# Hybrid encoder trunk on one core: first norm of the mixer row by row, and four other moves in the mixer's order of work

## The chip, the cores and the metric

One core of one Trainium2 chip runs the whole program once. The metric is device time in microseconds (us), the median of three runs. TensorE (PE in the rows) does matmuls, PEld its weight loads, VectorE is DVE, ScalarE is ACT, GpSimd is POOL, and SyncE (SP) issues the DMAs.

## The reference, cut to what matters

Two sequences (512 and 1024 rows of 1024 features) go through one layer: feed-forward, mixer, feed-forward, each followed by a residual and a layer norm. The mixer has three groups side by side: a gated recurrence (256 features), differential attention (4 heads), and a Fourier mixing (256 features).

```python
def encoder_trunk(x, ...):
    x = layer_norm(ALPHA * x + 0.5 * swiglu(x, ffn1_wg[l], ffn1_wu[l], ffn1_wd[l]), ln_g[l, 0], ln_b[l, 0])
    x = layer_norm(ALPHA * x + hybrid_mixer(x, w_in[l], ...), ln_g[l, 1], ln_b[l, 1])
    x = layer_norm(ALPHA * x + 0.5 * swiglu(x, ffn2_wg[l], ffn2_wu[l], ffn2_wd[l]), ln_g[l, 2], ln_b[l, 2])
def diff_attention(q, k, v, lam, subln_g, lam_init):
        s = jnp.einsum('bqhcd,bkhcd->bhcqk', qi, k) * scale + bias[None, :, None]
        p = jax.nn.softmax(s, axis=-1)
        w = p[:, :, 0] - lam * p[:, :, 1]
        return jnp.einsum('bhqk,bkhe->bqhe', w, v)
    o = o * lax.rsqrt(jnp.mean(o * o, -1, keepdims=True) + NORM_EPS) * subln_g * (1.0 - lam_init)
def fourier_mix(f):
    out = jnp.fft.fft2(fg, axes=(1, 3), norm='ortho').real
```

## The kernel before, in words

The rows are split into three chunks of 512: chunk 0 is the short sequence (q=0), chunks 1 and 2 are the long one (q=1). `ffn` runs before and after the mixer; the change touches only the mixer, which takes the span from about 1050 to 1745 us. Nearly all products are made in three passes of split operands: `mm3` (L139) issues three matmuls, and `split` makes a rounded part on ACT (L133) and the rest on DVE (L134).

**Two interleaved streams.** `attention` is a generator with one step per block of 128 queries: 16 blocks for q=0 (4 heads of 4), then 32 for q=1 (4 heads of 8). `others` is the second stream, a chain of generators: 18 steps left of the input projection `project` (each 24 matmuls of 128x512), mixed with the two Fourier generators `fnet` (7 and 12 steps), then `out_proj` of chunk 0, `first_norm`, and `out_proj` of chunk 1. `along` (L96) advances `others` after attention step n until its count of steps is at least `int(PACE(n))`. Before, PACE is 2 + 2.4 n up to n = 14 and grows by 0.8 a step from there. Step 0 comes before the first block, so n is also the block's number.

**One attention block** n: fill `ahead` with scores up to two blocks further (three in q=1; LOOK); one `next` on each tail of earlier `values`; `weigh` (L1061 to L1069) mixes both softmax maps and transposes the weights; then RATE[q] steps of the next head's `load` (8 in q=0, 1 in q=1); every second block starts a `values` tail. A load has seven DMAs of q, k and v. Scores are 8 matmuls (L1040, q=1), a bias and minimum on DVE (L1043) and an exp on ACT (L1045). A `values` tail has three steps, one a block: the product with v (L1077) and copies (L1080, L1081); column sums of squares (L1087), L1088 and a power on POOL (L1089); transposes of the result (L1093), the scaling (L1094), a split and the write to `y` in DRAM.

**The rest of the order.** `fnet` makes products with a channel table `ct`, then one group of 12 matmuls for each table tile; `table()` loads one tile ahead into one of two `r` slots. `out_proj(c)` loads eight tiles of `y` as soon as they are marked in `mixed` (else it yields a step that does nothing), then takes 16 steps of 24 matmuls. For chunk 0 it goes beside attention and writes its rows to `x1p` in DRAM. `first_norm` (one step) loads the four rows of `x1p` into `x` slots and calls `layer_norm` (L204): all four rows together on ACT, DVE and POOL, among them two `tensor_add` on POOL (L230). `layer_norm_row` (L236) is the row-wise form that the other norms use.

A planner places the instructions: on each engine it may put an instruction that it takes to be ready ahead of an earlier one. Tiles come from tagged slots (`xt` 6, `w` 5, `x` 6, `a` 5, `p`, `b`, `d`, `r` 2, `m` 4); a new tile waits until a slot of its tag is free, its DMA on SP's queue among others. "any" walks through a, x and p (13 slots), "any_b" alternates b and d. PSUM has three `big` and two `mm` slots in the mixer. The two score maps of a block and a projection step both take `big`.

Of the kernel before, what the change touches and what calls it, by code (L numbers as in the profile page):

```python
# [20 lines left out]
P = 128  # L21
# [18 lines left out]
FIRST = 30  # L40
PACE = lambda n: 2 + 2.4 * n + max(0, n - 14) * (0.8 - 2.4)
AHEAD = {(q, h): 2 + ((q, h) == (9, 2)) for q in range(2) for h in range(HEADS)}
RATE = (8, 1)
STORE = lambda nc, t: nc.sync
FN = 256
BATCH = 4
POOLED = lambda t: t % 2 == 0
MIXER = lambda nc, q, qb: nc.vector
# [26 lines left out]
def f32(ap):  # L75
    return ap.bitcast(F32)
# [27 lines left out]
class Kernel:  # L104
# [93 lines left out]
    def ln_params(self, i, tag):  # L198
# [3 lines left out]
        return ps  # L202

    def layer_norm(self, rows, sums, params, dst=None, part=range(TPC)):  # L204

        nc = self.nc
        for t0 in part[::BATCH]:
            ts = range(t0, min(t0 + BATCH, part.stop))
            n = len(ts)
            st = self.tiny("st", [3, TPC])[:, :, :n]  # L210
            mean, var, rs = (st[:, i] for i in range(3))
            if sums.shape[2] > 1:
                nc.vector.tensor_reduce(mean, sums[:, t0:t0 + n], axis=mybir.AxisListType.X, op=ALU.add)
                nc.vector.tensor_scalar(mean, mean, -1.0 / D, None, op0=ALU.mult)
            else:
                nc.vector.tensor_scalar(mean, sums[:, t0:t0 + n, 0], -1.0 / D, None, op0=ALU.mult)
            for t in ts:
                k = t - t0
                nc.scalar.activation(self.slot("a", [D], BF16), rows[t], AF.Square, bias=mean[:, k:k + 1],
                                     accum_out=var[:, k:k + 1])  # L220
            nc.vector.tensor_scalar(var, var, 1.0 / D, EPS / ALPHA ** 2, op0=ALU.mult, op1=ALU.add)
            nc.gpsimd.tensor_tensor(rs, var, self.mhalf[:, :n], op=ALU.pow)
            for t in ts:
                a, k = rows[t], t - t0
                nc.vector.scalar_tensor_tensor(a, a, mean[:, k:k + 1], params[0], op0=ALU.add, op1=ALU.mult)  # L225
            for t in ts:
                a, k = rows[t], t - t0
                if POOLED(t):
                    nc.scalar.activation(a, a, AF.Identity, scale=rs[:, k:k + 1])
                    nc.gpsimd.tensor_add(a, a, params[1])  # L230
                else:
                    nc.vector.scalar_tensor_tensor(a, a, rs[:, k:k + 1], params[1], op0=ALU.mult, op1=ALU.add)  # L232
                if dst is not None:
                    STORE(nc, t).dma_start(dst[t], a)

# [749 lines left out]
    def attention(self, blocks, dist, others):  # L985
# [85 lines left out]
        def values(q, h, qc):  # L1071
            NB = SEQS[q] // P
            zz, wt = chunks.pop((q, h, qc))
            vv = packs[q, h][2]
            po = self.psum("mm", [QC])
            for kb in range(NB):
                nc.tensor.matmul(po, vv[:, kb, :], wt[:, kb, :], start=kb == 0, stop=kb == NB - 1)  # L1077
            o = self.slot("any_b", [2, QC])
            o, sq = o[:, 0], o[:, 1]
            nc.scalar.copy(o, po)  # L1080
            nc.scalar.square(sq, po)  # L1081
            ms = self.tiny("ms", [2, JQ])
            nc.vector.scalar_tensor_tensor(ms[:, 0], zz[:, :, 0], EPS, zz[:, :, 0], op0=ALU.mult, op1=ALU.mult)
            yield
            pb = self.psum("mm", [QC])
            for j in range(JQ):
                nc.tensor.matmul(pb[:, j:j + 1], sq[:, j * P:(j + 1) * P], self.ones, start=True, stop=True)  # L1087
            nc.vector.scalar_tensor_tensor(ms[:, 0], pb[:, 0:JQ], 1.0 / P, ms[:, 0], op0=ALU.mult, op1=ALU.add)  # L1088
            nc.gpsimd.tensor_tensor(ms[:, 1], ms[:, 0], self.mhalf[:, 0:JQ], op=ALU.pow)  # L1089
            yield  # L1090
            pb = self.psum("mm", [QC])
            for j in range(JQ):
                nc.tensor.transpose(pb[:, j * P:(j + 1) * P], ms[:, 1, j:j + 1].to_broadcast([P, P]), self.ident)  # L1093
            nc.vector.scalar_tensor_tensor(o, o, self.subg, pb, op0=ALU.mult, op1=ALU.mult)  # L1094
            y = self.slot("any_b", [2, QC], F32R)
            self.split(y[:, 0], y[:, 1], o)
            nc.sync.dma_start(f32(self.scr["y", q, 2 + h])[:, :, qc * QC:(qc + 1) * QC].rearrange("a p s -> p a s"), f32(y))
            self.mixed[q, 2 + h, qc * QC] = 1
# [6 lines left out]
        for n, block in enumerate(blocks):  # L1105
            q, h, qb = block
            i = heads.index((q, h))
            while len(ahead) <= LOOK[q] and n + len(ahead) < len(blocks):
                block = blocks[n + len(ahead)]
                run(loads[heads.index(block[:2])])  # L1110
                ahead.append(scores(*block))
            for tail in tails:
                next(tail, None)
# [11 lines left out]
    def fnet(self, q, S):  # L1125
# [3 lines left out]
        H, N = S // 2, FN  # L1129
        ct = self.slot("any", [2, 2 * P], F32R)  # L1130
        nc.sync.dma_start(f32(ct), f32(self.scr["chan", q]).rearrange("a p n -> p a n"))
# [21 lines left out]
        else:  # L1153
            abs_ = self.slot("xt", [2, 2, S // P, 2 * P], F32R)
            abs_ = [abs_[:, cb] for cb in range(2)]
        abs_ = [[ab[:, l] for l in range(2)] for ab in abs_]
        for cb in range(2):
            fs, ab = ahead, abs_[cb]
# [8 lines left out]
        ys = [[self.slot("any", [S], F32R) for _ in range(2)] for _ in range(2)]  # L1167
        parts = fourier_parts(S)
        order = [t for tiles, _, _ in parts for t in tiles]
        tabs = []  # L1170

        def table():
            if order:
                tabs.append(self.slot("r", [2, 2, N], F32R))
                nc.sync.dma_start(f32(tabs[-1]), f32(self.scr["dft", q])[order.pop(0)])

        table()
        for tiles, sl, mirror in parts:
            if mirror:
                pss = [self.psum("mm", [2, N]) for _ in range(2)]  # L1180
            else:
                both = self.psum("mm", [2, N])
                pss = [both[:, cb:cb + 1] for cb in range(2)]
            for t in tiles:
                table()
                tab = tabs.pop(0)
                for cs in range(2):
# [22 lines left out]
    def out_proj(self, c, src, accs, beside=None):  # L1210
# [4 lines left out]
        if beside:  # L1215
            pairs = [self.slot("w", [2, 2, CH], F32R) for _ in range(2)]
            four = self.slot("xt", [KD // 2, 2, CH], F32R)
            yt = [p[:, i] for p in pairs for i in range(2)] + [four[:, i] for i in range(4)]
        else:
# [102 lines left out]
    def mixer(self, project, x1, x2, x1p, chunk):  # L1322
# [16 lines left out]
        def first_norm():  # L1339
            self.layer_norm(self.load_rows(x1p, "x"), self.sums[:, 0], self.ln_params(1, "x"), chunk(x2, 0))  # L1340
            yield

        def begun(steps):
# [4 lines left out]
        others = Steps(islice(project, 15), begun(fnets[0]), project, islice(fnets[0], 3), begun(fnets[1]), *fnets,  # L1348
                       self.out_proj(0, chunk(x1, 0), None, beside=x1p), first_norm(),
                       self.out_proj(1, chunk(x1, 1), accs[1]))  # L1350
        along(self.attention(blocks[0] + blocks[1], dist, others), others, PACE)
# [68 lines left out]
```

## Time and profile before

| | us |
|---|---|
| median of 3 runs (2820.43 to 2826.11) | 2821.38 |
| the profiled execution's own time | 2823.13 |
| its span, first to last instruction | 2821.3 |
| PE busy (97%) | 2739.7 |
| DVE busy (68%) | 1920.5 |
| ACT busy (41%) | 1153.8 |
| POOL busy | 104.6 |

Busy time is a share of the whole span; a stage's limit is read from the windows. "<-" in a wait names what ended it. PEclk is TensorE's granted clock as a share of full speed; in single stretches it is 1.00 (2.4 GHz) or 0.5 (1.2 GHz), and a window shows the mean.

### The profile page before, as it was taken

The numbers are of one execution on the slowest core, as the hardware profiler recorded it, in microseconds if no ns is written. First come the engines' busy times: TensorE is split into PE (matmuls) and PEld (weight loads), VectorE is DVE, ScalarE is ACT, GpSimd is POOL, SyncE is SP. The second block draws the span as 40 slices with busy tenths as digits, with TensorE's granted clock in tenths as the row PEclk, the third lists the DMA queues.
The fourth block names the chain that finished last, engine by engine and source line by source line (L and its number), as shares of the span: only waits on it lengthen the run. The fifth ranks groups of instructions, "written<-read, shape, count | busy, mean of one in ns | idle before, by whom it ended". The sixth has DMA issues, their size and how long they took to land. (4 is left out here: it accounts for less than half of the span.)

```text
span 2821.3 us, 39205 instructions
## 1 busy us (share of the span) xinstructions
PE 2739.7 (97%) x14940; PEld 2505.0 (89%) x14940; DVE 1920.5 (68%) x3218; ACT 1153.8 (41%) x2155; POOL 104.6 (4%) x104
## 2 busy tenths in 40 slices
PE   7999999999999999999988989999999999999998
PEld 7998999899999987987867979999999999999997
DVE  7677767686767773453477774877776668676677
ACT  5344434333323243663356562544433334232323
POOL 2000000010000010000000010000000001000001
PEclk9999999999999999999999999999999999999999
DMA  7799866888655573225577566488876577555553
GB/s 248 262 303 313 296 244 248 308 297 270 239 194 194 180 234 106 96 103 168 168 229 194 154 215 235 162 293 272 303 276 239 216 291 283 194 187 189 199 181 111
DMA packets 302284, 627.40 MB, mean 222 GB/s; under 512 B 22544, under 2 KB 178832, under 8 KB 283152
## 3 DMA queue, kind: packets, MB, share of 16 engines
q1 hardware_dynamic: 298096, 618.09, 63.7%
q0 software_dynamic: 4000, 6.82, 0.9%
q8 instruction: 117, 1.92, 0.3%
q14 instruction: 71, 0.58, 0.1%
HBM read 388.90 MB, written 235.93 MB: 221 GB/s over the span
## 5 line engine op out<-in xcount | busy, mean ns | idle before, releaser
L139 PE MATMUL up<-xt,a 128*128 128x384 f32 x4032 | 734.0, 337 | 2.9 <-DVE xt L134 2.1
L139 PEld LDWEIGHTS up<-xt,a 128*128 128x128 f32 x4032 | 701.8, 188 | 13.5 <-DVE xt L134 2.8
L139 PE MATMUL up<-xt,w 128*128 128x384 f32 x3360 | 617.5, 337 | 0.0
L139 PEld LDWEIGHTS up<-xt,w 128*128 128x128 f32 x3360 | 588.8, 188 | 21.4 <-ACT t L462 8.9
L139 PE MATMUL big<-w,h 128*128 128x512 f32 x1584 | 387.3, 393 | 1.9 <-ACT h L133 1.6
L586 DVE SCALAR_TENSOR_TENSOR x<-big,x 128x512 f32<-128x512 f32 x420 | 278.9, 685 | 107.1 <-PE big L139 104.3
L139 PEld LDWEIGHTS big<-w,h 128*128 128x128 f32 x1584 | 295.0, 188 | 60.7 <-ACT h L133 3.4
L139 PE MATMUL big<-a,h 128*128 128x512 f32 x1260 | 319.9, 395 | 2.4 <-ACT h L133 2.4
L139 PEld LDWEIGHTS big<-a,h 128*128 128x128 f32 x1260 | 234.9, 189 | 44.1 <-ACT h L133 2.8
L139 PE MATMUL big<-xt,w 128*128 128x512 f32 x1008 | 235.0, 392 | 5.8 <-issue 2.7
L533 DVE SCALAR_TENSOR_TENSOR x<-big,x 128x1024 f32<-128x1024 f32 (+1 forms) x156 | 177.2, 1139 | 87.0 <-PE big L139 86.9
L139 PEld LDWEIGHTS big<-xt,w 128*128 128x128 f32 x1008 | 189.2, 189 | 47.3 <-issue 3.1
L134 DVE TENSOR_TENSOR a<-w,a 128x512 fp32r<-128x512 f32 x244 | 164.4, 688 | 70.4 <-ACT a L133 65.7
L133 ACT CAST a<-w 128x512 fp32r<-128x512 f32 x244 | 148.0, 621 | 25.7 <-DMA w<-in_ffn_wg 11.9
L134 DVE TENSOR_TENSOR a<-b,a 128x512 fp32r<-128x512 f32 x176 | 121.5, 694 | 42.4 <-ACT a L133 39.8
L133 ACT CAST a<-b 128x512 fp32r<-128x512 f32 x176 | 108.6, 620 | 97.0 <-PE up L139 38.9
L133 ACT CAST h<-t 128x384 fp32r<-128x384 f32 x168 | 86.1, 513 | 125.8 <-DVE t L516 79.7
L139 PE MATMUL mm<-w,xt 128*128 128x256 f32 x960 | 122.2, 286 | 0.1
L139 PEld LDWEIGHTS mm<-w,xt 128*128 128x128 f32 x960 | 118.4, 193 | 0.6 <-DVE x L1244 0.5
L512 ACT ACTIVATE t<-t 128x384 f32<-128x384 f32 x132 | 69.3, 525 | 81.4 <-DVE t L457 42.1
L462 ACT COPY t<-up 128x384 f32<-128x384 f32 x84 | 40.3, 479 | 152.0 <-PE up L139 151.9
L443 DVE TENSOR_TENSOR t<-t,up 128x384 f32<-128x384 f32 x84 | 46.3, 552 | 82.2 <-ACT t L442 82.1
(329 smaller groups left out, 3046.6 us busy)
## 6 DMA issues: line engine op xcount, KB each, us to landing
left<-a SPq DMA_DIRECT2D x280, 512.0 KB, 4.2
w<-left SPq DMA_DIRECT2D x136, 1024.0 KB, 4.7
w<-in_ffn_wg SPq DMA_DIRECT2D x23, 1024.0 KB, 5.6
w<-in_ffn_wu SPq DMA_DIRECT2D x23, 1024.0 KB, 7.6
d<-in_ffn_wd SPq DMA_DIRECT2D x88, 256.0 KB, 4.3
x<-x SPq DMA_DIRECT2D x44, 512.0 KB, 4.1
ops<-a SPq DMA_DIRECT2D x42, 512.0 KB, 3.6
w<-in_ffn_wd SPq DMA_DIRECT2D x20, 1024.0 KB, 5.0
```

The source lines that it names most:

```text
L133: self.nc.scalar.copy(hi, src)
L134: self.nc.vector.tensor_sub(lo, src, f32(hi))
L139: self.nc.tensor.matmul(out, lhs(l), rhs(r), start=first and n == 0, stop=last and n == 2, skip_group_check=onto)
L443: nc.vector.tensor_add(s, s, b)
L462: nc.scalar.copy(s2 := quarter(), a)
L512: nc.scalar.activation(g, x, AF.Silu)
L533: nc.vector.scalar_tensor_tensor(accs[t][:, at], pd, scale, accs[t][:, at], op0=ALU.mult, op1=ALU.add, **acc)
L586: nc.vector.scalar_tensor_tensor(x, ps, scale, x, op0=ALU.mult, op1=ALU.add)
```

## The change

1. `first_norm` uses the row-wise norm, one row loaded ahead into `m` slots, and advances one step for every step of `out_proj` of chunk 1 (`together`). 2. RATE of q=1 becomes 2. 3. Two Fourier tables are loaded ahead, in slots r, r, m, the first two before the channel products; `ct` moves from "any" to `m`. 4. The last step of a `values` tail comes one block later, and its two working tiles and its result share one "any_b" tile. 5. The three scores of the first block are separated by yields, and PACE starts with three slower steps. Besides, `out_proj` of chunk 0 takes four single slots (m, m, m, any) in place of one `xt` slot.

```diff
-PACE = lambda n: 2 + 2.4 * n + max(0, n - 14) * (0.8 - 2.4)
+RAMP = 3
+PACE = lambda n: 2 + min(n, RAMP) + 2.4 * max(0, n - RAMP) + max(0, n - RAMP - 14) * (0.8 - 2.4)
-RATE = (8, 1)
+RATE = (8, 2)
+TABLES = "rrm"
...
-    def layer_norm(self, rows, sums, params, dst=None, part=range(TPC)):
...
 def values(q, h, qc):
-            o = self.slot("any_b", [2, QC])
-            o, sq = o[:, 0], o[:, 1]
+            y = self.slot("any_b", [2, QC], F32R)
+            sq, o = f32(y[:, 0]), f32(y[:, 1])
...
             nc.gpsimd.tensor_tensor(ms[:, 1], ms[:, 0], self.mhalf[:, 0:JQ], op=ALU.pow)
             yield
+            yield
...
-            y = self.slot("any_b", [2, QC], F32R)
...
                 ahead.append(scores(*block))
+                if n == 0:
+                    yield
...
 def fnet(self, q, S):
-        ct = self.slot("any", [2, 2 * P], F32R)
+        ct = self.slot("m", [2, 2 * P], F32R)
...
+        tabs, tags = [], cycle(TABLES)
+
+        def table():
+            if order:
+                tabs.append(self.slot(next(tags), [2, 2, N], F32R))
+                nc.sync.dma_start(f32(tabs[-1]), f32(self.scr["dft", q])[order.pop(0)])
+
+        table()
+        table()
         for cb in range(2):
...
             for t in tiles:
+                tab = tabs.pop(0)
                 table()
-                tab = tabs.pop(0)
...
 def out_proj(self, c, src, accs, beside=None):
-            four = self.slot("xt", [KD // 2, 2, CH], F32R)
-            yt = [p[:, i] for p in pairs for i in range(2)] + [four[:, i] for i in range(4)]
+            yt = [p[:, i] for p in pairs for i in range(2)] + [self.slot(t, [2, CH], F32R) for t in ("m", "m", "m", "any")]
...
         def first_norm():
-            self.layer_norm(self.load_rows(x1p, "x"), self.sums[:, 0], self.ln_params(1, "x"), chunk(x2, 0))
-            yield
+            params = self.ln_params(1, "x")
+            load = lambda t: self.load_rows([x1p[t]], "m")
+            xs = load(0)
+            yield
+
+            def rows():
+                for t in range(TPC):
+                    if t + 1 < TPC:
+                        xs.extend(load(t + 1))
+                    yield xs.pop(0), self.sums[:, 0, t], chunk(x2, 0)[t]
+
+            yield from self.layer_norm_rows(rows(), params)
+
+        def together(steps, others):
+            for _ in steps:
+                next(others, None)
+                yield
+            run(others)
...
-                       self.out_proj(0, chunk(x1, 0), None, beside=x1p), first_norm(),
-                       self.out_proj(1, chunk(x1, 1), accs[1]))
+                       self.out_proj(0, chunk(x1, 0), None, beside=x1p),
+                       together(self.out_proj(1, chunk(x1, 1), accs[1]), first_norm()))
```

## Rows read from the trace of the kernel before

**Rows 1.** The page: span, and busy time of TensorE and VectorE.

```profile
span 2821.3 us, 39205 instructions
PE 2739.7 (97%) x14940; PEld 2505.0 (89%) x14940; DVE 1920.5 (68%) x3218; ACT 1153.8 (41%) x2155; POOL 104.6 (4%) x104
```

**Rows 2.** Windows of the mixer: start:end, length, busy time by engine, clock, DMA.

```profile
1286.00:1296.00 10.00, 5.85 (x22) 3.58 (x21) 6.84 (x21) 6.38 (x15) 0.00 (x0) 0.93 0.80 207
1296.00:1318.00 22.00, 22.00 (x94) 18.03 (x94) 5.47 (x7) 4.21 (x6) 0.00 (x0) 0.96 0.40 123
...
1405.00:1441.00 36.00, 26.57 (x168) 22.16 (x169) 25.37 (x63) 20.51 (x49) 2.48 (x3) 0.96 0.69 203
1441.00:1481.00 40.00, 35.95 (x221) 31.31 (x221) 29.09 (x64) 23.07 (x45) 0.69 (x1) 0.95 0.80 239
1481.00:1499.00 18.00, 17.26 (x93) 14.16 (x92) 16.36 (x39) 15.14 (x28) 2.39 (x3) 1.00 0.89 246
1499.00:1514.00 15.00, 8.48 (x32) 6.59 (x33) 6.07 (x9) 4.56 (x8) 0.59 (x1) 0.77 0.84 222
...
1658.50:1677.50 19.00, 11.36 (x60) 8.66 (x57) 15.51 (x16) 14.03 (x23) 9.24 (x4) 0.98 0.75 274
1677.50:1701.50 24.00, 18.73 (x78) 14.50 (x79) 11.81 (x26) 9.58 (x16) 2.10 (x3) 0.71 0.82 248
1701.50:1745.00 43.50, 43.50 (x355) 43.50 (x354) 13.96 (x36) 6.70 (x7) 0.00 (x0) 0.97 0.78 269
```

**Rows 3.** Waits of TensorE from 1286 to 1745: total us, times, longest.

```profile
PE mm L1093 <- POOL ms L1089: 7.5, 6, 3.4
PE big L1040 <- DMA xt<-qk: 5.9, 2, 4.8
...
PE mm L139 <- DMA r<-dft: 3.5, 2, 2.6
```

**Rows 4.** The page's group of projection matmuls: busy us, mean ns.

```profile
L139 PE MATMUL big<-xt,w 128*128 128x512 f32 x1008 | 235.0, 392 | 5.8 <-issue 2.7
```

**Rows 5.** Timeline: VectorE's mix, and TensorE's longest wait for POOL.

```profile
1439.52 0.75 DVE L1064 SCALAR_TENSOR_TENSOR a<-a,mx 128x512 f32<-128x512 f32 x1
...
1440.87 0.69 PE L1093 MATMUL mm<-ident,ms 128*128 128x128 f32 x2 [3.37 <-POOL ms L1089]
```

**Rows 6.** Timeline: the second long head's last k load, and TensorE's wait for it.

```profile
1498.86 0.58 SPq L1013 DMA_DIRECT2D xt<-qk  x1
...
1507.60 5.72 PE L1040 MATMUL big<-xt 128*128 128x512 f32 x13 [4.79 <-DMA xt<-qk]
```

**Rows 7.** The first norm by line, and one ACT line of the row-wise norm: min/median/max ns.

```profile
L222 POOL TENSOR_TENSOR st<-st,mhalf x1: 1977/1977/1977, 1665.4 to 1665.4; 128x4 f32<-128x4 f32 x1
L225 DVE SCALAR_TENSOR_TENSOR x<-x,st x4: 1273/1274/1276, 1665.2 to 1668.8; 128x1024 f32<-128x1024 f32 x4
L230 POOL TENSOR_TENSOR x<-x x2: 3293/3306/3318, 1669.0 to 1672.3; 128x1024 f32<-128x1024 f32 x2
L232 DVE SCALAR_TENSOR_TENSOR x<-x,st x2: 3355/3370/3384, 1670.0 to 1673.3; 128x1024 f32<-128x1024 f32 x2
L245 ACT ACTIVATE a<-x,st x32: 1134/1149/1155, 551.6 to 2812.7; 128x1024 bf16<-128x1024 f32 x32
```

**Rows 8.** Timeline of TensorE: the parts of a long block with no filler.

```profile
1490.92 2.09 PE L1040 MATMUL big<-xt 128*128 128x512 f32 x8
1493.53 3.62 PE L1077 MATMUL mm<-xt 128*128 128x256 f32 x16
1496.99 1.04 PE L1067 MATMUL big<-ident,x 128*128 128x128 f32 x8
```

**Rows 9.** Timeline of TensorE: the end of attention.

```profile
1694.96 3.72 PE L1077 MATMUL mm<-xt 128*128 128x256 f32 x16 [0.51 <-ACT xt L1069]
1699.49 0.61 PE L1087 MATMUL mm<-ones,d 128*128 128x1 f32 x4 [0.80 <-ACT d L1081]
1701.19 0.69 PE L1093 MATMUL mm<-ident,ms 128*128 128x128 f32 x2 [1.09 <-POOL ms L1089]
```

More of the change, by code (lines that the diff above doesn't have):

```diff
@@ L40 @@
 FIRST = 30
-PACE = lambda n: 2 + 2.4 * n + max(0, n - 14) * (0.8 - 2.4)
+RAMP = 3
+PACE = lambda n: 2 + min(n, RAMP) + 2.4 * max(0, n - RAMP) + max(0, n - RAMP - 14) * (0.8 - 2.4)
 AHEAD = {(q, h): 2 + ((q, h) == (9, 2)) for q in range(2) for h in range(HEADS)}
-RATE = (8, 1)
-STORE = lambda nc, t: nc.sync
+RATE = (8, 2)
+TABLES = "rrm"
 FN = 256
-BATCH = 4
-POOLED = lambda t: t % 2 == 0
 MIXER = lambda nc, q, qb: nc.vector
@@ L202, in ln_params @@
         return ps
-    def layer_norm(self, rows, sums, params, dst=None, part=range(TPC)):
[L206 to L234, printed above, removed]
     def layer_norm_row(self, a, sums, params, dst):
@@ L1156, in fnet @@
         abs_ = [[ab[:, l] for l in range(2)] for ab in abs_]
+        parts = fourier_parts(S)
+        order = [t for tiles, _, _ in parts for t in tiles]
+        tabs, tags = [], cycle(TABLES)
[5 more added lines that the diff above has]
+        table()
         for cb in range(2):
@@ L1167, in fnet @@
         ys = [[self.slot("any", [S], F32R) for _ in range(2)] for _ in range(2)]
[L1168 to L1177, printed above, removed]
         for tiles, sl, mirror in parts:
```

## The prediction

> **What bounds the kernel now.** I read the page first: TensorE is busy 97% of the span, 2739.7 of 2821.3 us [rows 1]. So only two things can be won here: the time in which TensorE waits, and the time in which it runs at half clock. The change adds and removes no matmul. The windows of the mixer come next [rows 2]; the reader should subtract TensorE's busy time from the length, and multiply what is missing of the clock by the length (at 1.2 GHz half of the time is lost). Four places stand out:
>
> - A, the first scores, 1286 to 1318: idle 10.0 - 5.85 = 4.2 us; clock 0.07 x 10 + 0.04 x 22 = 1.6 us.
> - B, the Fourier mixing beside the short sequence, 1405 to 1481: idle 9.4 + 4.05 = 13.5 us; clock 0.04 x 36 + 0.05 x 40 = 3.4 us.
> - C, the second long head, 1499 to 1514: idle 6.5 us; clock 0.23 x 15 = 3.5 us.
> - D, the first norm and the end of attention, 1658.5 to 1701.5: idle 7.6 + 5.3 = 12.9 us; clock 0.02 x 19 + 0.29 x 24 + 0.03 x 43.5 = 8.7 us.
>
> Together 37.1 us of waits and 17.2 us of clock, 54 us: the ceiling. Third come the waits [rows 3], to see which part of the change meets which gap.
>
> **A: scores apart.** Before, three pairs of scores stand behind each other, each needs a `big` slot that VectorE must empty, and nothing lies between. Now one step of `others` lies after each: a projection chunk of 24 matmuls x 235.0/1008 us = 5.6 us [rows 4], which is longer than the whole wait of 4.2 us. These chunks are not new work; they are drawn forward, and what they leave uncovered is priced in B. Of the 5.8 us I take 4.5; bounds 0 (a chunk takes `big` too, so it can queue for the same slot) and 5.8.
>
> **B: tables and the output norm.** TensorE waits 3.5 us for tables [rows 3]. Two ahead, with the first pair issued four or eight steps before use, these go. The table loads still stand on SyncE's queue; a third one waits for the slot of the tile just used, and y stores and head loads stand behind it, as behind one today. The wait for POOL's power (3.37 us at 1440.87 [rows 5]) moves one block back. But VectorE's mix for the next transposes ends only at 1439.52 + 0.75 = 1440.27, so without that wait TensorE would still have stood until then: 0.6 us are sure, 3.4 possible, I take 1.5. The tail that moves carries two transposes, two VectorE instructions, one cast and one store on SyncE; `mixed` is marked one block later, which costs `out_proj` of chunk 0 two empty steps (below). With shorter gaps I take half of the clock, 1.7. Against this: the filler ends sooner. PACE plus the three new yields puts `others` at 5 + 2.4 k after block k, three steps more than today (2 + 2.4 k), so the last projection chunk falls in block 6, not 8, and one or two more short blocks have Fourier steps alone. In this stretch 13.5 us are idle over some nine blocks, 1.5 each; I charge 2.7. Net 3.5 + 1.5 + 1.7 - 2.7 = 4. Bounds: -3 (charge of two blocks, nothing but tables minus new waits) and 13.
>
> **C: head loads two per block.** The k load issued at 1498.86 was awaited until 1507.6 [rows 6]; the two waits for q and k loads sum to 5.9 us [rows 3], and the clock lost 3.5. At one per block, seven load steps begin at block 17 and block 22 needs them (three ahead of block 25): five are out by then, two are issued at the last moment. At two per block all are out in block 20, two blocks early. A block without filler takes 2.09 + 1.04 + 3.62/2 us and some 0.4 of small matmuls, 5.3 us [rows 8], so the lead is 10 us, against the 8.7 us from that issue to the end of the wait. Also `out_proj` no longer holds an `xt` slot, which both tiles of a load need. Gain 8 of 9.4; bounds 0 (the load waits for `xt` on SyncE's queue) and 10.
>
> **D: the norm by rows.** Today VectorE makes 4 x 1.27 us, then 2 x 3.37 us while POOL's two adds of 3.3 us run beside it; 11.8 us stand in front of the scores' minima, and TensorE runs dry [rows 7]. After: two VectorE instructions a row of 1.27 us (10.2 us in all), on ACT one of 1.15 us and some small ones, on POOL four powers for one and no add, on SyncE the same four loads, two parameter loads and four stores. Where do they lie? `others` counts 18 projection and 19 Fourier steps; 38 to 43 are the loads of `out_proj` of chunk 0 with two empty steps (its last tile is marked in block 20), 44 to 59 its matmuls, the norm from 60. The new count is 38.6 + 0.8 (k - 14): 60 is reached in block 41, and the last block, 48, reaches 65. So six of the norm's ten steps lie in the last eight blocks and the rest beside `out_proj` of chunk 1. Is there room? A stretch of blocks without filler shows VectorE 16.36 of 18 us, ACT 15.14, TensorE 17.26 [rows 2]: TensorE still sets the pace. Blocks 41 to 45 take 5 x 5.3 = 26.5 us and leave VectorE 9% of that, 2.4 us; two row instructions fall there, 2.5 us. The last three blocks have no scores and leave more. So the rows fit. What stays is the chain at the end, 0.51 + 0.80 + 1.09 = 2.4 us [rows 9], some 3 us of single waits beside the rows, and about 5 us of clock. 21.6 - 10.4 = 11. Bounds 4 (the clock stays as it is and half the waits return) and 18.
>
> Here a rule speaks against the change. Row: four VectorE instructions ran at 1.27 us beside POOL's power of 1.98 us, no longer than elsewhere, while those beside POOL's adds took 3.37 [rows 7]. So I charge the four powers nothing. The Trainium skill, SBUF — State Buffer, section Who interferes with whom, says that a VectorE instruction with two SBUF inputs and a GpSimd instruction that reads SBUF exclude each other for a whole instruction. By that, each of the three added powers could hold VectorE for the row's 1.98 us, and the sum would be worse by up to 6 us; the power's row does not bear that out.
>
> **Sum.** 4.5 + 4 + 8 + 11 = 27.5 us. The profiled execution took 2823.13 us, 1.8 above the median of 2821.38; 2823.1 - 27.5 = 2795.6 there, so 2794 for the median. The bounds add to +1 and +47, which do not come together; four terms of which each may miss by half leave about 12 to either side.
>
> **Rivals.**
>
> 1. *VectorE takes over.* In B it is busy 54.5 of 76 us, and in blocks without filler 91%. Then a gap closed in one place opens in the next block, and only waits go behind which no engine works: tables 3.5 and head loads 5.9 us, 9.4. Time 2812. For it: the wait in rows 5 was VectorE's work as much as POOL's. Against: in D and C VectorE itself stood idle or ran stretched instructions. Chance 0.17.
> 2. *Short waits keep the clock down.* The clock fell in B after a run of waits of which the longest was 3.4 us, and the change leaves eight blocks at the end of attention without filler, where today there are seven (42 to 48). Then the waits go, but the 10 us of clock in my sum (1.3 in A, 1.7 in B, 3.4 in C, 3.7 in D) stay lost: 2804. Against: 18 us of such blocks ran at clock 1.00 [rows 2]. The Trainium skill, TensorE: Matmul & The Clock Gate, section A second HAM failure mode: psum-queue depth-cycling, says that frequent small waits between groups of matmuls suffice to bring the clock down; by that rule this case would hold, and the 18 us speak against it. Chance 0.12.
> 3. *Slower: the tail runs out of score slots.* Attention holds eight of the 13 a, x and p slots for scores ahead, nine at a change. The norm's parameters now hold two x from block 41 to the end, its squares one a, and one "any" is held by `out_proj`: nine are left. If that is one too few, scores are no longer ahead and every block waits for its own chain. The price is that of 1658.5 to 1677.5, where the norm blocks the scores: 7.6 us of waits on 11.4 of work [rows 2], 0.67. Eight blocks of 5.3 us then wait 28 us, and the clock loses 7 (0.29 x 24) once more; 3 us of waits are in my sum already: 2794 + 32 = 2826. It decides when fewer than eight slots are left. Against: today's norm takes six x slots and one a, and even so the loss was 21.6 us, with the norm's burst in it. Chance 0.09.
> 4. *Nearly all goes:* the ceiling of 54 us, 2768. It needs an end of attention with no wait, which [rows 9] exclude for 2.4 us. Chance 0.05.
>
> That the change doesn't do what it says is within rival 1: the planner may already place filler between the scores as far as slots allow, and A is then 0.
>
> **The numbers.** The forecast holds 0.57, between 2782 and 2806. A measurement of this kernel can tell 0.2%, 5.6 us, from no change: faster is below 2815.7. The forecast, rivals 2 and 4 and most of rival 1 (0.13 of 0.17) lie there: 0.87. Rival 1's other 0.04 and 0.02 of rival 3 make 0.06 of no change; 0.07 slower. From 2778 to 2813 the range holds the forecast, rival 2 and most of rival 1.
>
> **What would show it.** A: TensorE's busy time in the window of the first scores is full, with matmuls into `big<-xt,w` between those of L1040. B: no wait of L139 for `dft`, hardly one of L1093 for POOL. C: no wait of L1040 for `qk`. D: L249 and L251 at 1.27 us spread from block 41 on, L232 and L230 gone, the clock at 1.00 but for a stretch before `out_proj` of chunk 1. I am wrong if TensorE's busy time falls by less than 10 us while its waits stay (rival 1), if long waits for VectorE's L1043 stand in the last eight blocks (rival 3), or if waits on SyncE for b, d or `xt` slots hold loads that TensorE awaits.

## The result, and the profile after

The changed kernel takes 2803.16 us (median of 6 runs, 2797.28 to 2806.49); the kernel before took 2822.31 us in the 6 runs beside it (2820.43 to 2826.11). The ratio is 0.9927, 95% interval 0.9916 to 0.9937: faster by 19.2 us, where 27.5 were forecast. Sign and range held, the size was 8 us too large. The profiled execution took 2802.54 us, 0.6 below its median, so the traces can be compared directly. First the page of the changed kernel, span and busy time:

```profile
span 2800.8 us, 39195 instructions
PE 2735.3 (98%) x14940; PEld 2502.8 (89%) x14940; DVE 1919.9 (69%) x3221; ACT 1152.8 (41%) x2161; POOL 100.0 (4%) x105
```

Against [rows 1] the span is 20.5 us shorter and TensorE's busy time 4.4 us shorter. With the same 14940 matmuls, that is 16.1 us less waiting and 4.4 us less time lost to the clock. Where? Windows of the changed kernel (start:end, length, busy by engine, granted clock, DMA):

```profile
1040.00:1140.00 100.00, 93.56 (x423) 76.50 (x422) 43.67 (x55) 41.10 (x59) 5.99 (x6) 0.97 0.41 129
...
1280.00:1392.00 112.00, 111.44 (x501) 90.31 (x500) 39.47 (x89) 32.87 (x66) 1.40 (x2) 1.00 0.54 167
1392.00:1480.00 88.00, 74.48 (x443) 63.36 (x443) 64.45 (x152) 51.60 (x111) 4.39 (x5) 0.92 0.81 235
1480.00:1530.00 50.00, 47.99 (x291) 41.62 (x290) 38.16 (x80) 32.27 (x55) 3.71 (x4) 1.00 0.68 185
...
1640.00:1750.00 110.00, 103.59 (x755) 97.14 (x754) 67.15 (x133) 47.09 (x84) 11.88 (x13) 0.97 0.78 271
```

The kernel before, cut at the same times (these cuts hold the four places of [rows 2] in both kernels, though the changed kernel is some us further on):

```profile
1040.00:1140.00 100.00, 93.72 (x434) 77.04 (x433) 43.89 (x55) 44.13 (x62) 5.67 (x6) 1.00 0.41 131
...
1280.00:1392.00 112.00, 107.50 (x478) 86.48 (x477) 40.33 (x95) 34.59 (x72) 1.57 (x2) 0.98 0.54 164
1392.00:1480.00 88.00, 74.32 (x441) 62.67 (x440) 59.52 (x142) 46.98 (x102) 3.98 (x5) 0.96 0.70 208
1480.00:1530.00 50.00, 42.74 (x234) 35.98 (x235) 37.03 (x75) 30.07 (x50) 3.68 (x4) 0.93 0.73 208
1640.00:1750.00 110.00, 97.09 (x638) 87.67 (x637) 58.86 (x115) 44.69 (x70) 12.54 (x9) 0.92 0.73 248
```

Idle is length less TensorE's busy time; lost clock is what is missing of 1.00, times the length. Idle plus lost clock, before and after:

| place | before | after | gain | forecast |
|---|---|---|---|---|
| start of the mixer, 1040 to 1140 | 6.3 + 0 | 6.4 + 3.0 | -3.1 | none |
| A, first scores, 1280 to 1392 | 4.5 + 2.2 | 0.6 + 0 | 6.1 | 4.5 |
| B, Fourier mixing, 1392 to 1480 | 13.7 + 3.5 | 13.5 + 7.0 | -3.3 | 4 |
| C, second long head, 1480 to 1530 | 7.3 + 3.5 | 2.0 + 0 | 8.8 | 8 |
| D, end of attention, 1640 to 1750 | 12.9 + 8.8 | 6.4 + 3.3 | 12.0 | 11 |

The sum is 20.5 us, the difference of the spans. Three of the four terms came in a little above the forecast; B came out on the other side of zero, and one loss lies at the mixer's start, where none of the four terms lies. The two columns of a place can overlap: while TensorE waits, a low clock costs nothing. In B after the change the mean clock inside the 6.4 us wait below is 0.67, so 2.1 of the 7.0 us are counted twice.

What is left shows in TensorE's waits from 1286 to 1745 (total us, times, longest):

```profile
PE big L138 <- ACT w L132: 6.4, 1, 6.4
PE mm L1061 <- POOL ms L1056: 2.8, 2, 1.7
PE big L1007 <- DVE mx L1010: 2.8, 3, 1.9
```

The three groups of [rows 3] were 7.5 us for POOL, 5.9 for the loads of q and k, 3.5 for tables. POOL is down to 2.8, the other two are gone. The longest wait is a new one, 6.4 us for a piece of the second fold.

**A.** TensorE's timeline at the first scores: matmuls of a projection (L138, `big<-xt,w`) between the scores (L1007), and no wait.

```profile
1289.96 0.39 PE L1007 MATMUL big<-w,a 128*128 128x512 f32 x1
1290.19 1.75 PE L138 MATMUL big<-xt,w 128*128 128x512 f32 x7
1291.77 0.39 PE L1007 MATMUL big<-w,a 128*128 128x512 f32 x1
1292.00 1.07 PE L138 MATMUL big<-xt,w 128*128 128x512 f32 x4
```

**B.** The new wait, followed back through the timeline of SyncE, VectorE, ScalarE and TensorE, with SyncE's waits for a table slot and for the data of a y store, from the view of waits from 1400 to 1480:

```profile
SPq L1133 <- PE mm L138: 22.0, 5, 11.8
...
SPq L1175 <- ACT a L132: 4.8, 1, 4.8
```

```profile
1422.06 0.44 SPq L1175 DMA_DIRECT2D y<-a  x1
1422.60 1.26 SPq L1133 DMA_DIRECT2D r<-dft  x2
1423.95 0.46 SPq L1104 DMA_DIRECT2D a<-f  x1
...
1430.43 0.69 DVE L1105 TENSOR_TENSOR x<-a 128x512 f32<-128x512 f32 x1 [3.45 <-DMA a<-f]
...
1432.21 0.41 ACT L132 CAST w<-a 128x256 fp32r<-128x256 f32 x1 [4.39 <-DVE a L1109]
...
1432.67 0.80 PE L138 MATMUL big<-m,w 128*128 128x256 f32 x2 [6.43 <-ACT w L132]
```

The load of `f` for the second fold stands on SyncE's queue behind the stores of y and two table loads, is issued at 1423.95, and lands for VectorE at 1430.43. TensorE stands idle from 1426.23 on (the end of its previous entry, 1425.50 + 0.73). Of the 22.0 us that SyncE waited for table slots, 20.7 come after this load; ahead of it stands the store that waited 4.8 us for its data. The same chain before:

```profile
1429.01 0.32 SPq L1135 DMA_DIRECT2D a<-f  x1
...
1434.18 0.69 DVE L1136 TENSOR_TENSOR x<-a 128x512 f32<-128x512 f32 x1 [0.62 <-DMA a<-f]
...
1442.07 3.21 PE L139 MATMUL big<-x,w 128*128 128x256 f32 x15
```

There `f` was issued 13.1 us before TensorE used the fold. Now TensorE is ready for it 2.3 us after the issue.

**C.** SyncE issues the second head's last two k loads from 1485.06 to 1486.55 (the last one went out at 1498.86 in [rows 6]). TensorE's longest wait there is 1.10 us for a copy of ScalarE, and all 14 matmuls of the scores run behind it:

```profile
1485.06 1.49 SPq L980 DMA_DIRECT2D xt<-qk  x2
```

```profile
1502.32 3.71 PE L1007 MATMUL big<-xt 128*128 128x512 f32 x14 [1.10 <-ACT xt L1036]
```

**D.** The first norm by line, 1640 to 1700 (ns min/median/max, first and last start), the counterpart of [rows 7]:

```profile
L216 DVE SCALAR_TENSOR_TENSOR m<-m,st,x x4: 1271/1278/1284, 1648.7 to 1671.9; 128x1024 f32<-128x1024 f32 x4
...
L218 DVE SCALAR_TENSOR_TENSOR m<-m,st,x x4: 1276/1282/1284, 1650.5 to 1674.9; 128x1024 f32<-128x1024 f32 x4
...
L214 POOL TENSOR_TENSOR st<-st,mhalf x4: 549/557/1223, 1649.9 to 1667.9; 128x1 f32<-128x1 f32 x4
```

The pairs of 3.37 and 3.31 us are gone. The rows still lie closer than forecast: row 0 at 1648.7, the other three between 1662.4 and 1676.2. One of them shows in the timeline, put between the minimum and the mix of a block:

```profile
1667.48 1.28 DVE L216 SCALAR_TENSOR_TENSOR m<-m,st,x 128x1024 f32<-128x1024 f32 x1
1668.67 1.28 DVE L1031 SCALAR_TENSOR_TENSOR a<-x,mx,a 128x1024 f32<-128x1024 f32 x1
...
1670.01 0.55 PE L1034 MATMUL big<-ident,a 128*128 128x128 f32 x3 [2.05 <-DVE a L1031]
```

### The profile page after: what moved, and what is told of

Its sections match the earlier page's. It is cut to its first block, busy times and chain, and to the rows that moved or that the text cites. A ratio compares the mean times of both kernels' runs of the same rounds, so it can differ in the third digit from the quotient of the medians.

```text
span 2800.8 us, 39195 instructions
## 1 busy us (share of the span) xinstructions
PE 2735.3 (98%) x14940; PEld 2502.8 (89%) x14940; DVE 1919.9 (69%) x3221; ACT 1152.8 (41%) x2161; POOL 100.0 (4%) x105
## 4 chain that ended last, share of the span: by engine, by line
PE 71%; issue 18%; DVE 5%; DMA 3%; ACT 1%; POOL 1%; SPq 0%; POOLq 0%; DVEq 0%; ACTq 0%
PE up L138 31%; PE big L138 28%; PE mm L138 5%; PE mm L1044 2%; PE big L1007 2%; PE big L1034 1%; PE big L257 1%; DVE a L133 1%; DMA dft<-b 1%; DMA w<-in_ffn_wg 1%; POOL st L214 1%; DVE x L218 1%; DVE x L216 0%; DVE xt L133 0%; DMA x<-x 0%
## 5 line engine op out<-in xcount | busy, mean ns | idle before, releaser
L138 PE MATMUL up<-xt,a 128*128 128x384 f32 x4032 | 733.5, 336 | 2.4 <-DVE xt L133 1.5
L138 PEld LDWEIGHTS up<-xt,a 128*128 128x128 f32 x4032 | 701.3, 188 | 13.1 <-ACT a L132 2.3
L138 PE MATMUL up<-xt,w 128*128 128x384 f32 x3360 | 617.6, 337 | 0.0
L138 PEld LDWEIGHTS up<-xt,w 128*128 128x128 f32 x3360 | 589.0, 188 | 21.5 <-ACT t L429 8.9
L138 PE MATMUL big<-w,h 128*128 128x512 f32 x1584 | 388.7, 394 | 3.0 <-ACT h L132 2.7
L138 PEld LDWEIGHTS big<-w,h 128*128 128x128 f32 x1584 | 296.1, 188 | 62.1 <-ACT h L132 4.6
L138 PE MATMUL big<-a,h 128*128 128x512 f32 x1260 | 319.9, 395 | 2.0 <-ACT h L132 2.0
L138 PEld LDWEIGHTS big<-a,h 128*128 128x128 f32 x1260 | 234.6, 188 | 43.7 <-ACT h L132 2.4
L138 PE MATMUL big<-xt,w 128*128 128x512 f32 x1008 | 237.4, 393 | 6.2 <-issue 3.3
L138 PEld LDWEIGHTS big<-xt,w 128*128 128x128 f32 x1008 | 190.1, 190 | 48.2 <-issue 3.7
L133 DVE TENSOR_TENSOR h<-t,h 128x384 fp32r<-128x384 f32 x168 | 92.6, 553 | 10.4 <-ACT h L132 10.3
L214 POOL TENSOR_TENSOR st<-st,mhalf 128x1 f32<-128x1 f32 x36 | 43.5, 1210 | 1557.3 <-ACT st L213 1552.8
```

The lines of the kernel that those rows point to most:

```text
L133: self.nc.vector.tensor_sub(lo, src, f32(hi))
L138: self.nc.tensor.matmul(out, lhs(l), rhs(r), start=first and n == 0, stop=last and n == 2, skip_group_check=onto)
L214: nc.gpsimd.tensor_tensor(rs, var, self.mhalf[:, :1], op=ALU.pow)
```

## The experiments

Every run is the changed kernel with one edit (two in el_x and u_xt_rate, none in after2), timed beside the kernel before. The changed kernel itself stands at 2803.16 us, 0.9927.

| run | us (median, lowest to highest) | ratio to before, 95% |
|---|---|---|
| m_late | 2801.84 (2798.76 to 2807.99) | 0.9922, 0.9909 to 0.9935 |
| u_tables | 2806.47 (2803.47 to 2809.33) | 0.9936, 0.9924 to 0.9949 |
| u_pace | 2803.87 (2801.42 to 2809.47) | 0.9929, 0.9915 to 0.9942 |
| u_rate | 2807.12 (2804.55 to 2811.46) | 0.9941, 0.9929 to 0.9954 |
| e_x | 2796.24 (2793.17 to 2799.94) | 0.9900, 0.9885 to 0.9916 |
| el_x | 2802.56 (2799.11 to 2806.04) | 0.9921, 0.9906 to 0.9935 |
| u_first | 2817.49 (2810.21 to 2821.76) | 0.9973, 0.9962 to 0.9983 |
| u_outnorm | 2802.66 (2797.54 to 2805.72) | 0.9921, 0.9906 to 0.9935 |
| u_xt | 2800.49 (2796.89 to 2803.93) | 0.9919, 0.9905 to 0.9933 |
| u_xt_rate | 2805.67 (2803.53 to 2806.08) | 0.9934, 0.9922 to 0.9946 |
| after2 | 2803.99 (2796.45 to 2810.93) | 0.9929, 0.9913 to 0.9945 |
| e_x2 | 2800.88 (2798.61 to 2802.38) | 0.9918, 0.9904 to 0.9932 |

**u_first: the first norm as before, in one burst.** It takes `layer_norm` and the old `first_norm` back.

```diff
-            yield from self.layer_norm_rows(rows(), params)
+            self.layer_norm(self.load_rows(x1p, "x"), self.sums[:, 0], self.ln_params(1, "x"), chunk(x2, 0))
+            yield
```

> The changed kernel with the first norm of before: one step, four rows together in x slots, POOL's two adds. Theory 1 (the burst of the norm on VectorE and its x slots stopped the scores): waits of 10 us or more and some 14 us at half clock return at the end of attention; slower than the changed kernel by 10 to 14 us, about 2815. Rival (the norm by rows only spreads the same waits, and the gain at the end comes from elsewhere): within 3 us of 2803.

Measured 14 us over the changed kernel, and one wait at the end of attention (waits of u_first from 1640 to 1705, then its window):

```profile
PE big L1069 <- DVE mx L1045: 12.7, 1, 12.7
```

```profile
1640.00:1750.00 110.00, 91.72 (x630) 85.40 (x628) 56.00 (x115) 44.84 (x73) 14.58 (x9) 0.89 0.68 236
```

TensorE stands 12.7 us until VectorE is through the norm and reaches the scores' minima. Of 110 us, 18.3 are idle and 12.1 lost to the clock, against 6.4 and 3.3: this part carries the largest share of the gain. The windows differ by 20.7 us and the times by 14, in part because the mean clock is 0.57 in the 12.7 us of the wait itself, where it costs nothing (5.5 us).

**u_rate: head loads one per block again.**

```diff
-RATE = (8, 2)
+RATE = (8, 1)
```

> The changed kernel with one load step per long block again. Theory 1 (the load of the second long head was late because of the rate): a wait of TensorE for q and k loads of 4 to 6 us comes back near the second long head, with 3 us of clock: slower than the changed kernel by 6 to 9 us (2809 to 2812). Rival (it was the shortage of xt slots, which the single slots of the output projection have ended): no wait for these loads, equal within 2 us.

Measured 4 us over, and the intervals of the two kernels overlap. No wait for k at the second head is named any more. TensorE waits instead for the first weights of `out_proj`, whose load went out at 1497.91 (1493.06 in the changed kernel). But the last k load is late again. Timelines of SyncE and TensorE in u_rate, and the window of C:

```profile
1497.91 0.41 SPq L144 DMA_DIRECT2D r<-in_w_out  x1
...
1498.92 0.58 SPq L980 DMA_DIRECT2D xt<-qk  x1
...
1505.31 0.50 PE L1007 MATMUL big<-xt 128*128 128x512 f32 x1 [1.10 <-ACT xt L1036]
1507.88 0.78 PE L138 MATMUL mm<-w,m 128*128 128x256 f32 x2 [2.07 <-ACT w L132]
...
1511.87 2.76 PE L1007 MATMUL big<-xt 128*128 128x512 f32 x6
```

```profile
1480.00:1530.00 50.00, 45.37 (x255) 39.01 (x254) 37.00 (x77) 30.30 (x52) 4.24 (x5) 0.93 0.64 176
```

That load is issued at 1498.92 (1498.86 in [rows 6]) and lands 10.2 us later, at 1509.1. Where the changed kernel runs 14 matmuls of the scores in one piece at 1502.32, one runs here at 1505.31 and the others come from 1511.87 on, behind a step of `out_proj`. So most of the old gap is back under another name: a stretch of 6.83 us at half clock follows, and the window is idle for 4.6 us and loses 3.5 to the clock, against 2.0 and 0 in the changed kernel and 7.3 and 3.5 before. That is 6.1 of C's 8.8 us. There are also waits of 0.65 and 2.46 us for q and k of the first long head.

**u_xt: `out_proj` holds an `xt` slot again.**

```diff
-            yt = [p[:, i] for p in pairs for i in range(2)] + [self.slot(t, [2, CH], F32R) for t in ("m", "m", "m", "any")]
+            four = self.slot("xt", [KD // 2, 2, CH], F32R)
+            yt = [p[:, i] for p in pairs for i in range(2)] + [four[:, i] for i in range(4)]
```

> The changed kernel with the xt slot of before for four y tiles of the output projection (chunk 0), instead of m, m, m and any. Theory 1 (at two steps a block the loads of the second long head are early enough by themselves): no wait of TensorE for q and k loads after 1490 us, equal within 2 us of the changed kernel. Theory 2 (the freed xt slot is what lets these loads go): their last issue falls to about 1498 us or later, a wait of 3 to 6 us for q and k loads comes back there, slower by 4 to 8 us.

Equal in time, and the last head load goes out at 1491.29, as early as without the edit (1492.49). The freed slot gives nothing.

**u_xt_rate: both of these edits together.**

> Both undone: the xt slot of before and one load step a block. Either theory: if the head loads' gap of before (4.8 us in one wait, 6.8 us at half clock) is made by these two alone, it returns here in full, and the kernel is slower than the changed one by 7 to 10 us. If the earlier end of the Fourier steps (the new pace) already cures it, the wait stays below 2 us and the time within 4 us of the kernel with one load step alone (2807).

Measured 2805.67, within the spread of u_rate and 2.5 us over the changed kernel. The window of C in u_xt_rate:

```profile
1480.00:1530.00 50.00, 44.59 (x251) 38.48 (x250) 35.77 (x73) 27.51 (x46) 2.11 (x3) 0.93 0.64 164
```

Idle 5.4 us and 3.5 lost to the clock: 6.9 of C's 8.8 us are gone again. No wait for k is named here either; the wait for weights is there (2.67 us, with 6.83 us at half clock), though they were issued at 1493.86 and landed in 8.8 us, much as in the changed kernel (1493.06, 9.3 us). What differs is the last k load, issued at 1494.92 and landed 10.2 us later, at 1505.1; all but one of the scores' matmuls come from 1507.73 on. Both runs with one load step a block lose most of C's gain in C's own window, so the rate is what closes this gap. In the whole time the medians show 4.0 and 2.5 us of it, inside the spread.

**m_late: the two first tables issued after the second fold's load.**

```diff
-        table()
-        table()
         for cb in range(2):
             fs, ab = ahead, abs_[cb]
             if cb == 0:
                 ahead = folded(1)
+                table()
+                table()
```

> The changed kernel with the first two table loads of each Fourier generator issued after the second fold's load of f instead of before it. Theory 1 (SyncE's order): in the changed kernel the load of f stood behind a table load that waited for its slot, so the fold came late, TensorE waited 6.4 us in one piece and then ran 13.65 us at half clock; with the order turned round that wait is below 1 us, at least half of the half-clock stretch goes, and the time falls by 7 to 12 us, to about 2792 to 2796. Theory 2 (the Fourier stretch is limited by VectorE and by missing filler): the wait comes back under another name within the same 80 us, and the time stays within 3 us of 2803.

The load of `f` went out at 1422.30, only 1.6 us earlier, since the y stores ahead of it still wait for their data. The wait shrank by about as much (timeline of m_late):

```profile
1430.11 1.68 PE L138 MATMUL big<-m,w 128*128 128x256 f32 x6 [4.58 <-ACT w L132]
```

The half-clock stretch fell from 13.65 to 6.83 us, and the idle time from 1392 to 1480 to 10.9 us. The median is 1.3 us lower, inside the spread. So the tables on the queue are 1.9 of the 6.4 us, not the whole of it. In time Theory 2 holds.

**e_x: the second `f` of the long sequence loaded at the start, into an x slot.**

```diff
         ahead = folded(0)
+        late = None
+        if S > CH:
+            late = self.slot("x", [S])
+            nc.sync.dma_start(late, self.scr["f", q][1])
...
-                ahead = folded(1)
+                ahead = folded(1, late)
```

(`folded` takes `late` as its `f` and issues no load then.)

> The changed kernel with one load drawn forward: the second f of the long sequence is loaded when its Fourier generator begins (into an x slot), ahead of the table loads and of the y stores of the short sequence on SyncE's queue; the folds stay where they are. Theory 1 (TensorE's 6.4 us wait and the 13.65 us at half clock come from that load's place on the queue): the wait for the fold falls below 1 us, half-clock time in the Fourier stretch falls to 6.8 us or less, and the time to 2790 to 2797. Theory 2 (the stretch has too little other work, and a wait closed there opens again under another name): the wait for the fold goes all the same, but TensorE's idle time between 1392 and 1480 us stays above 11 us and the time within 4 us of 2803.

The wait for the fold is down to 1.4 us, and others have opened. TensorE's waits in e_x from 1392 to 1480, and the window:

```profile
PE mm L138 <- DMA r<-dft: 2.8, 1, 2.8
PE big L1007 <- DMA xt<-qk: 2.3, 2, 1.4
PE big L138 <- ACT w L132: 1.4, 1, 1.4
```

```profile
1392.00:1480.00 88.00, 75.01 (x427) 63.01 (x426) 64.13 (x150) 50.56 (x111) 3.44 (x5) 0.90 0.86 244
```

Idle 13.0 us, as in the changed kernel with its 13.5, and the clock is 0.90 without the long wait. The time was 7 us lower, which that window does not explain, so both were run again.

**after2 and e_x2: the changed kernel and e_x once more, side by side.**

> The changed kernel once more, beside the next one on the same chip: 2800 to 2806 us.

> The kernel with the second f loaded early, once more beside the changed kernel. Theory 1 (the load of f stood too late on the queue): faster than the changed kernel by 4 to 8 us again. Rival (the first result was the spread of single runs, since the idle time of the Fourier stretch did not fall): equal within 2 us.

2803.99 against 2800.88 us. The intervals of the ratios overlap, and e_x2 is idle for 14.1 us from 1392 to 1480, at a clock of 0.94. e_x was the lower of the two both times, by 7 and by 3 us; a gain of a few us is possible, and is not shown.

**el_x: e_x and m_late together.**

> The last kernel with, besides, the first two table loads after the second fold. Theory 1: as the last one within 2 us, since the load of f has already passed them. Theory 2: within 4 us of 2803.

2802.56 us. The fold's wait is 1.4 us, but a load of q or k is now awaited for 5.0 us and a table for 3.1; idle 15.5 us. Two cures are no better than either.

**u_tables: one table ahead, as before.** `table()` and its first call move back behind the channel products, every table takes an `r` slot, and only one is on its way.

```diff
-        table()
-        table()
...
+        table()
...
-                tab = tabs.pop(0)
                 table()
+                tab = tabs.pop(0)
```

> The changed kernel with the tables loaded one ahead, in r slots alone and after the channel products, as before the change. Theory 1: the 6.4 us wait for the fold goes (the f load has no waiting table load ahead of it), waits for tables of 3 to 4 us come back, and with less time at half clock the kernel is faster than the changed one by 3 to 8 us (2795 to 2800). Theory 2 and the prediction's term for the tables: slower than the changed kernel by 3 to 4 us (about 2807).

3.3 us over the changed kernel, close to the term of 3.5, but the intervals overlap and the way there was another: the wait for tables is only 0.36 us, the fold's wait is gone, and waits of 2.80 us for VectorE's minima and 2.63 us for q or k stand instead. Idle from 1392 to 1480 is 13.5 us again, and the clock 0.92, though the long wait is gone.

**u_pace: the old pace, and no step between the first scores.**

```diff
-PACE = lambda n: 2 + min(n, RAMP) + 2.4 * max(0, n - RAMP) + max(0, n - RAMP - 14) * (0.8 - 2.4)
+PACE = lambda n: 2 + 2.4 * n + max(0, n - 14) * (0.8 - 2.4)
...
-                if n == 0:
-                    yield
```

> The changed kernel without the yields between the first three scores and with the old pace. Theory 1 (part 5 closes the gap at the first scores): waits of some 4 us and a short half-clock stretch come back near 1290 us, and the filler ends later, which gives 1 to 3 us back in the Fourier stretch; in all slower than the changed kernel by 2 to 5 us (2805 to 2808). Rival (the three steps drawn forward cost as much filler later as they cover): equal within 2 us.

2803.87 us, equal. The windows of u_pace show why (its profiled execution, 2809.47 us, is the slowest of the five, so only these places are read from it):

```profile
1280.00:1392.00 112.00, 107.29 (x474) 86.42 (x473) 40.36 (x91) 33.59 (x69) 1.51 (x2) 0.97 0.57 171
1392.00:1480.00 88.00, 77.81 (x449) 66.94 (x448) 57.75 (x140) 44.99 (x98) 3.60 (x5) 0.94 0.66 192
```

At the first scores 4.7 us of idle time and 3.4 of clock are back; in the Fourier stretch idle is 10.2 us instead of 13.5, clock 0.94 instead of 0.92. A's gain is real in its place (7.5 us by this run), and 5.1 us of it are paid for in B, where the filler drawn forward is missing. The run undoes pace and yields together, so their shares stay open.

**u_outnorm: the output norm over one block, as before.**

```diff
             yield
-            yield
             pb = self.psum("mm", [QC])
```

> The changed kernel with the last step of the output norm one block earlier again (the shared tile stays). The prediction's term: TensorE's waits for POOL's power return, 3 to 4 us in all in the Fourier stretch, of which VectorE hides half: slower by 1 to 3 us, about 2805. Rival (the moved step costs more, since the short sequence's last tile comes later and gives two empty steps): equal or faster by up to 3 us.

Equal, 2802.66 us. The waits for POOL's power are back in the view of waits of u_outnorm from 1286 to 1745:

```profile
PE mm L1060 <- POOL ms L1056: 7.6, 8, 1.9
```

That is 7.6 us against 2.8. But the fold's wait is 4.78 us instead of 6.43, and idle in B is 13.5 us with or without. The second block for the norm buys nothing that can be measured in the whole time.

## Why the prediction was right in sign and too large

The forecast split into 17.4 us of waits and 10.1 of clock; the spans give 16.1 and 4.4. So most of what was missing is clock. The time, 2803, is within 1 us of what rival 2 gave (2804), but not in rival 2's way: in A, C and D the clock gave 11.2 us back, where 8.4 were forecast, and it lost 3.5 in B and 3.0 at the mixer's start.

**A: gain as said (6.1 for 4.5), its price too low.** Full TensorE and `big<-xt,w` between the scores came as announced. The price belongs to B.

**B: the step that failed.** It said net +4; the windows give -3.3. The largest miss is the term for the clock: "With shorter gaps I take half of the clock, 1.7"; it lost 3.5 more instead. The waits gave 0.2 for 2.3. Two sentences behind these terms are wrong. "y stores and head loads stand behind it, as behind one today": what stands behind the tables is also the load of `f` for the second fold. And "I charge 2.7" for the filler that ends sooner was too little: with the old pace and no yields (u_pace) B loses 5.1 us less. The new pace brings that fold forward until TensorE is ready for it 2.3 us after its load is issued, where it had 13.1 us before; with the old pace (u_pace) the fold waits for 1.39 us. Out of it come 6.43 us of waiting. A half-clock stretch of 13.65 us (6.8 lost, before 6.83 and 3.4) lies over it and behind it, but that the wait makes it is not shown: u_tables has no wait for the fold and e_x one of 1.4 us, and their clock in B is 0.92 and 0.90, no higher than the changed kernel's 0.92. m_late puts 1.9 us of that wait on the tables' place in the queue. Beyond that, the runs that moved single waits in this stretch (m_late, e_x, el_x, u_tables, u_outnorm) left 10.9 to 15.5 us idle, the changed kernel 13.5, the kernel before 13.7. That is rival 1's sentence, a gap closed opens in the next, true in B alone. VectorE is busy there for 60 to 68 of 88 us, so it is not full; the view of waits names in turn loads, VectorE, ScalarE and POOL. The term for tables was right in number by luck (u_tables 3.3 of 3.5): without the tables ahead TensorE waits 0.36 us for them, and other waits make up the time. The term for the output norm (1.5) was worth nothing.

**C: right in mechanism and size (8.8 for 8).** With one load step a block the last k load is late again, and 6.1 (u_rate) and 6.9 us (u_xt_rate) of the gain are lost in this window, under the name of another wait. The freed `xt` slot, named beside the rate, is worth nothing (u_xt).

**D: right in mechanism and size (12.0 for 11).** u_first puts 14 us on the burst in the changed kernel; its windows lose more there than the kernel before did (30.4 for 21.7 us), so this is not the same sum as the 12.0. The 2.4 us chain of [rows 9] is now 0.75 + 1.09, and the waits from 1664 to 1682 sum to 6.1 us (0.54, 2.05, 1.70, 0.75, 1.09), where 2.4 + 3 were left in the sum; clock 3.3 for 5. That "the rest beside `out_proj` of chunk 1" would lie was wrong: all four rows end before attention's last wait at 1681.97, and three of them within 14 us.

The powers on POOL were charged nothing, against a rule. That VectorE is not held came true: the L216 that ran from 1667.48 to 1668.76 took 1.28 us although POOL computed two powers from 1667.41 to 1669.16, and the eight row instructions spread over 13 ns. What the prediction left out is the other direction, VectorE holding a power. Timelines of VectorE, POOL and TensorE at the end of attention:

```profile
1655.87 0.70 POOL L1056 TENSOR_TENSOR ms<-ms,mhalf 128x2 f32<-128x2 f32 x1 [5.41 <-DVE ms L1055]
...
1671.86 1.27 DVE L216 SCALAR_TENSOR_TENSOR m<-m,st,x 128x1024 f32<-128x1024 f32 x1
1672.08 1.61 POOL L1056 TENSOR_TENSOR ms<-ms,mhalf 128x2 f32<-128x2 f32 x1 [2.92 <-DVE ms L1055]
...
1673.74 0.69 PE L1061 MATMUL mm<-ident,ms 128*128 128x128 f32 x2 [1.70 <-POOL ms L1056]
```

Of the 24 powers of L1056 in the changed kernel, 20 took 0.69 to 0.74 us. The other four took 1.60 to 1.61; each was issued while VectorE ran a long instruction with two inputs in SBUF (the memory on the chip) and ended 0.5 to 0.6 us behind it (here 1673.69 behind 1673.13). TensorE waited for one of them, so a row of the norm costs about 0.9 us there (an estimate: 1.61 less 0.70). The Trainium skill, SBUF — State Buffer, section Who interferes with whom, says that two such instructions exclude each other; this trace agrees for POOL behind VectorE, and shows none of the eight row instructions held by a power.

**Rivals.** Rival 3 (score slots run out) shows nowhere: no wait for VectorE's minima stands in the last blocks, and the longest there is 2.05 us, for the mix. Rival 2 (the clock stays down) came in part: 10 us of clock were in my sum and 4.4 came in the whole trace. In e_x no wait of the Fourier stretch is over 2.8 us, and its clock is 0.90 there, below the 0.92 of the changed kernel with its 6.43 us wait (e_x2, the same kernel again, has 0.94). The Trainium skill, TensorE: Matmul & The Clock Gate, section A second HAM failure mode: psum-queue depth-cycling, says that short idle times between groups of matmuls are enough if they are frequent; that stretch of e_x agrees, and no run tests it by itself.

Of the signs of being wrong, half of the first came: TensorE's busy time fell by 4.4 us, less than 10, but its waits did not stay. The last came in another form: on SyncE's queue the load of `f` stood behind stores that waited for their data.

Reckoned by terms: 27.5 forecast, less 7.3 in B, plus 1.6, 0.8 and 1.0 in A, C and D, less 3.1 at the mixer's start (put at nothing; see the last section), is 20.5.

## What to carry to other kernels

Filler drawn forward to close one gap is taken from the place where it stood: price that place by the lead of each load used there (issue to use, 13.1 us before and 2.3 after), not by idle time per block. In a stretch where four engines and the loads end waits in turn, removing the longest wait moved the idle time and hardly lessened it (10.9 us at best, for 13.5); spend the effort where one instruction group is stretched or bunched, as the norm was (14 us). When a load is made earlier, read the whole queue around it: what is wanted soonest must not stand behind it.

## What was not expected

**A half-clock stretch near the mixer's start.** All 13 profiles of changed kernels have one, between 1066 and 1081, of 3.41 or 6.83 us, and six of them one more of 3.41 us between 1051 and 1060; the one profile of the kernel before has none there. The change does touch this place, though no matmul in it: with `ct` in an `m` slot, SyncE issues the load of the short sequence's channel table at 1062.52 (before, at 1364.6). It stands ahead of a load of projection weights, which goes out at 1064.81 (before, at 1064.58). TensorE's wait ahead of the stretch is 3.31 us, where it was 2.71. The six earlier stretches begin before this load goes out, so it cannot be behind those. No run moves `ct` back, and one profile of before cannot tell what comes and goes, so the cause stays open. The prediction had no term for it.

**One program has different half-clock stretches from run to run**: in B 13.65 us in the changed kernel's profile, 10.24 in after2's, which is the same kernel; the spans are 2800.8 and 2794.7 us. The runs of one kernel spread by 2.6 to 14.5 us, so gains of 2 to 3 us could not be settled.

**One power on POOL of 128x1 took from 0.54 to 2.54 us** (36 of them in the changed kernel, median 1.25). In the trace the length follows VectorE. The longest, issued at 2322.39, ended at 2324.94, 0.4 us behind the last of four VectorE instructions that ran back to back from 2321.71 to 2324.53, while the VectorE instructions of the rows at the end of attention kept to 1.27 to 1.28.
